# Token-major v projection with a gathered copy of n: residue copies, one warm-up matmul, one GpSimd subtraction, and a three-piece output store

## The chip, the cores and the metric

The kernel runs on one core of a Trainium2 chip. The metric is the device time of one execution in microseconds (us). Five engines work from queues of their own, each in its own order: TensorE (PE in the profile, with its weight loads as PEld), VectorE (DVE), ScalarE (ACT), GpSimd (POOL) and SyncE (SP), which only issues transfers here. SBUF is the on-chip memory of 128 partitions that all engines read; PSUM takes the results of matmuls.

## The reference

One layer of an encoder, for 512 tokens of width 1024, in float32. The part that matters here is the first norm and the combined projection, with v read out by strided subsequences for the dilated attention groups.

```python
n = rms_norm(h, norm_mix_pre[l])
proj = jnp.einsum('bsd,de->bse', n, w_in[l])
z_gmlp, q, k, v, gates = jnp.split(proj, split_points, axis=-1)
...
def strided(t):
    return t.astype(jnp.float32).reshape(B, L, dilation, H, Dh).transpose(0, 2, 1, 3, 4)
...
h = h + rms_norm(mix_out, norm_mix_post[l])
n2 = rms_norm(h, norm_mlp_pre[l])
hid = jnp.square(jax.nn.relu(jnp.einsum('bsd,df->bsf', n2, w_up[l])))
mlp_out = jnp.einsum('bsf,fd->bsd', hid, w_down[l])
h = h + rms_norm(mlp_out, norm_mlp_post[l])
```

There are three v groups of 512 columns. The first belongs to plain window attention; the second and the third are needed token by token within the residues r = 0..3 of the position modulo 4.

## The kernel before

**Arithmetic.** Every float32 product is made of three matmuls (`mm3`, lines 84 to 86): each operand is split into a high part (a rounded copy, made by ScalarE) and a low part (the difference, made by VectorE), and high x high, high x low and low x high are summed in PSUM.

**The start (lines 123 to 225).** x comes in four blocks of 128 tokens, shifted by 64 positions, in the order 1, 2, 3, 0. `square_x` takes the sum of squares of a block on ScalarE (line 169), `norm_x` scales the block on VectorE (`xn`, line 176), TensorE turns it in two groups of four transposes (`pt`, line 180), ScalarE copies the result into `nh` (line 182) and VectorE makes `nl` (line 183). So `nh` and `nl` hold n with the feature on the partition and the token along the row. Meanwhile the eight slabs of the first v group's weights are split: `w0hi` on ScalarE (line 193), `w0lo` on VectorE, for k = 3 and 7 on GpSimd (line 194). Each block then takes 24 matmuls into `pv`, 96 in all, and `pv` is split into `v0h` and `v0l`. Three unused matmuls (`idle`, line 153) and the two that spread the norm's gain (`pgn`, line 158) run before.

**The second and third v groups (`token_major`, lines 235 to 247, called at line 277).** For g = 0 and 1 and each residue r, the stationary operand is `n[:, k, ROT + r:ROT + S:4]`: 128 tokens, four apart, so that a partition reads 128 float32 numbers that stand 16 bytes apart. Each g takes 8 x 4 x 3 = 96 matmuls; the weights come as `slab` and are split into `hi` and `lo` (lines 74 and 75). Between them `four_sums` builds the sums of n that a later stage needs (`nf`, `sum`). The same `token_major` with unstrided stationary operands is used later for another column group.

**After that** come the projections of q and k for each head (`pf`), which take `nh` and `nl` as the moving operand, with the rotary part in `rope_tile`: the constants `rope`, `masks`, `perm`, `rows` and `wsp` are loaded through GpSimd's queue. Then follow the attention, the gates, the output projection and the feed-forward part.

**The end (lines 957 to 969).** For each of four blocks of tokens the last matmuls are followed by `post_norm`: squares on ScalarE (line 727), a small chain over VectorE and GpSimd for the scale, the products `y` (line 730), two sums of 128x512 into `o` (line 732), and two stores of 256 KB.

**What sets the order.** A scheduler fixes the order of each engine's instructions when the program is built; `tc.issue_after` adds constraints. At run time an engine that waits holds up everything behind it in its queue; only weight loads run ahead. Pools are stacked in SBUF: a pool that opens where another has closed waits for the last readers of the tiles it overlays.

Of the kernel before, what the change touches and what calls it, by code (L numbers as in the profile page):

```python
# [10 lines left out]
F32 = mybir.dt.float32  # L11
F32R = mybir.dt.float32r
AF = mybir.ActivationFunctionType
ALU = mybir.AluOpType
PSUM = bass.MemoryType.PSUM

P = 128
S = 512
D = 1024
KD = D // P  # L20
# [7 lines left out]
GW = 512  # L28
COL_U, COL_V = 0, GW
COL_Q, COL_K, COL_VV, COL_G = 1024, 2560, 4096, 5632  # L30
ROT = 64
# [5 lines left out]
def block_kernel(ctx: ExitStack, tc: tile.TileContext, x, norm_mix_pre, w_in, b_gate, ln_v_gain, ln_v_bias,  # L37
                 w_spatial, b_spatial, w_branch_a, w_branch_b, w_out, norm_mix_post, norm_mlp_pre, w_up,
                 w_down, norm_mlp_post, ident_c, rope_c, mask_c, perm_c, out):
    nc = tc.nc  # L40
    x, out, w_in, w_up, w_down, w_out = x[0], out[0], w_in[0], w_up[0], w_down[0], w_out[0]
    w_branch_a, w_branch_b, w_spatial = w_branch_a[0], w_branch_b[0], w_spatial[0]

    def pool(stack, name, bufs=1, space=None, side=None):
        kw = {"side": side} if side else {}
        if space is not None:
            kw["space"] = space
        return stack.enter_context(tc.tile_pool(name=name, bufs=bufs, reuse_waits="tile", **kw))
# [9 lines left out]
    onesq = consts.tile([P, P], F32, name="onesq")  # L58
# [47 lines left out]
    nh = npool.tile([P, KD, S + ROT], F32R, name="nh")  # L106
    nl = npool.tile([P, KD, S + ROT], F32R, name="nl")
# [3 lines left out]
    nat = slice(ROT, ROT + S)  # L111
# [7 lines left out]
    start = ExitStack()  # L119
# [3 lines left out]
    blocks = [1, 2, 3, 0]  # L123
# [18 lines left out]
    xts = [load_x(blocks[0])]  # L142
# [8 lines left out]
    for _ in range(3):  # L151
        idle = psA.tile([P, P], F32, name="idle", tag="acc", bufs=4)
        spun = nc.tensor.matmul(idle, onesq, onesq, start=True, stop=True)
    pgain = []
    for hf in range(2):
        pgn = psA.tile([P, 512], F32, name="pgn", tag=("y", "T")[hf])
        with tc.issue_after(spun.ins):
            spun = nc.tensor.matmul(pgn, onesq[:1], grow[:, hf * 512:(hf + 1) * 512], start=True, stop=True)
        pgain.append(pgn)

    def square_x(b, xt):
        junk = xpool.tile([P, D], F32, name="junk", bufs=1)
        ss = small.tile([P, 2], F32, name="ss")
        for hf in range(2):
            hs = slice(hf * 512, (hf + 1) * 512)
            if hf and b == blocks[0]:
                nc.vector.tensor_tensor_reduce(junk[:, hs], xt[:, hs], xt[:, hs], 1.0, 0.0, ALU.mult, ALU.add, ss[:, 1:2])
            else:
                sq = nc.scalar.activation(junk[:, hs], xt[:, hs], AF.Square, accum_out=ss[:, hf:hf + 1])
        return rstd_of(ss, 1.0 / D), sq  # L170
# [18 lines left out]
    def split_w0(k):  # L189
        raw = w0raw[k // 2][:, k % 2]  # L190
        hi = w0pool.tile([P, GW], F32R, name="w0hi")
        lo = w0pool.tile([P, GW], F32R, name="w0lo")
        ins = nc.scalar.activation(hi, raw, AF.Copy)
        (nc.gpsimd if k in (3, 7) else nc.vector).tensor_tensor(lo, raw, hi.bitcast(F32), op=ALU.subtract)
        w0.append((hi, lo))
        return ins

    rs = {0: square_x(blocks[0], xts[0])[0]}
    scaled, hi, lo = norm_x(blocks[0], xts[0], rs[0])
# [3 lines left out]
    with tc.issue_after(hi.ins):  # L203
        for k in range(2, 4):
            ins = split_w0(k)
        with tc.issue_after(ins.ins):
            rs[1], sq = square_x(blocks[1], xts[1])
        with tc.issue_after(sq.ins):
            for k in range(4, KD):
                ins = split_w0(k)  # L210
        with tc.issue_after(ins.ins):
            rs[2], sq = square_x(blocks[2], xts[2])
    for i in range(4):
        if i + 1 < 4:
            _, hi, lo = norm_x(blocks[i + 1], xts[i + 1], rs[i + 1])
        if i == 0:
            with tc.issue_after(hi.ins):
                rs[3], _ = square_x(blocks[3], xts[3])
        b = blocks[i]
        pv = psA.tile([P, GW], F32, name="pv", tag="acc", bufs=4)  # L220
        for k in range(KD):
            sl = slice(b * P, (b + 1) * P)
            mm3(pv, (nh[:, k, sl], nl[:, k, sl]), w0[k], k == 0, k == KD - 1)
        split_into(v0h[:, b], v0l[:, b], pv)
# [10 lines left out]
    def token_major(c0, stationary, evac, half_way=None):  # L235
        accs = [psA.tile([P, 512], F32, name="pv", tag="acc", bufs=4) for _ in range(4)]
        for k0, raw in slabs(w_in, c0, KD, 512, 4):
            if k0 and half_way:
                half_way()
            for j in range(0, 4, 2):  # L240
                wh, wl = wsplit(raw[:, j:j + 2])
                for jj in range(2):
                    k = k0 + j + jj
                    for r in range(4):
                        mm3(accs[r], (stationary(nh, k, r), stationary(nl, k, r)), (wh[:, jj], wl[:, jj]), k == 0, k == KD - 1)
        for r in range(4):
            evac(r, accs[r])
# [6 lines left out]
    def four_sums():  # L254
        with ExitStack() as st:
            spool = pool(st, "spool")
            f = spool.tile([P, KD, S], F32, name="nf")
            for k in range(0, KD, 2):
                nc.vector.tensor_tensor(f[:, k:k + 2], nhn[:, k:k + 2].bitcast(F32), nln[:, k:k + 2].bitcast(F32), op=ALU.add)
            fe, fo = f[:, 0:KD:2], f[:, 1:KD:2]  # L260
            nc.vector.tensor_tensor(fe[:, :, A], fe[:, :, A], fe[:, :, B], op=ALU.subtract)
            nc.vector.tensor_tensor(fe[:, :, B], fo[:, :, B], fe[:, :, B], op=ALU.subtract)
            nc.vector.scalar_tensor_tensor(fo[:, :, B], fe[:, :, A], -1.0, fo[:, :, B], op0=ALU.mult, op1=ALU.subtract)
            nc.vector.scalar_tensor_tensor(fo[:, :, A], fo[:, :, B], -1.0, fo[:, :, A], op0=ALU.mult, op1=ALU.subtract)
            for n, part in ((6, fo[:, :, B]), (5, fe[:, :, A]), (7, fe[:, :, B]), (4, fo[:, :, A])):
                hl = spool.tile([P, 2, KH, 256], F32R, name="sum", bufs=4)
                split_into(hl[:, 0], hl[:, 1], part)
                nc.gpsimd.dma_start(sums[n], hl)

    for g in range(2):  # L270
        def ev(r, ps, g=g):
            if r % 2:
                nc.vector.tensor_copy(v12[:, g, r], ps)
            else:
                nc.scalar.activation(v12[:, g, r], ps, AF.Copy)
        with tc.issue_after(hi.ins), tc.issue_after(lo.ins):
            token_major(COL_VV + (g + 1) * GW, lambda n, k, r: n[:, k, ROT + r:ROT + S:4], ev)
        if g == 0:
            four_sums()

    def feature_tile(wh, wl, nk, mh, ml, tag="acc"):
        ps = psA.tile([P, S], F32, name="pf", tag=tag, bufs={"acc": 4, "S": 2, "T": 1, "y": 1}[tag])
# [19 lines left out]
    for i, (vec, n) in enumerate(((b_gate, 16), (ln_v_gain, 4), (ln_v_bias, 4), (norm_mlp_pre, 8))):  # L302
        o = (0, 16, 20, 24)[i]
# [284 lines left out]
    for g2 in range(2):  # L588
        raw = wload([KD, 2 * P], lambda r: [(r, fcols(w_in, COL_U + g2 * 2 * P, KD, 2 * P))], "uw")
        for j in range(2):  # L590
            g = 2 * g2 + j
            wh, wl = wsplit(raw[:, :, j * P:(j + 1) * P], sub=nc.gpsimd)
            ps = psA.tile([P, S], F32, name="pf", tag="acc" if g else "T", bufs=4 if g else 1)
            for k in range(KD):
                ins = mm3(ps, (wh[:, k], wl[:, k]), (nhn[:, k], nln[:, k]), k == 0, k == KD - 1)
# [12 lines left out]
            t = gpool.tile([P, 4, P], F32, name="sv", bufs=2)  # L608
# [72 lines left out]
    for d in range(GSTD):  # L681
        g2 = gate_rows(d - GSTD)
        raw = gate_raw(d)
# [23 lines left out]
    gain = hpool.tile([P, D], F32, name="gain", bufs=1)  # L707
    nc.gpsimd.dma_start(gain, norm_mix_post.to_broadcast([P, D]))
    h2d = tc.dram_tile([S, D], F32, name="h2d")
    halves = [slice(0, 512), slice(512, 1024)]  # L710
# [10 lines left out]
    def all_banks():  # L721
        return [[psB.tile([P, 512], F32, name="pd", tag=tg, bufs=4) for _ in range(2)] for tg in ("tp", "tp", "acc", "acc")]

    def post_norm(pss, gain, ys, dst, res, junk):
        ss = small.tile([P, 2], F32, name="ss2")
        for hf, hs in enumerate(halves):
            nc.scalar.activation(junk[hf], pss[hf].rearrange("p (k c) -> p k c", c=P), AF.Square, accum_out=ss[:, hf:hf + 1])
            if hf:
                r = rstd_of(ss, 1.0 / D)
            nc.vector.tensor_tensor(ys[hf], pss[hf], gain[:, hs], op=ALU.mult)  # L730
        for hf, hs in enumerate(halves):
            nc.vector.scalar_tensor_tensor(dst[:, hs], ys[hf], r, res[:, hs], op0=ALU.mult, op1=ALU.add)

    wo = ExitStack()
    wopool = pool(wo, "wopool", bufs=5)
# [35 lines left out]
    for t in range(4):  # L771
        ts_ = slice(t * P, (t + 1) * P)
# [58 lines left out]
    for i in range(1, NSTD):  # L831
        raw = raw_up(i)
# [126 lines left out]
    for t in range(4):  # L959
        ts_ = slice(t * P, (t + 1) * P)  # L960
        h2 = n2pool.tile([P, D], F32, name="h2", tag="n2")
        nc.gpsimd.dma_start(h2, h2d[ts_])
        for hf in range(2):
            for f, hh, hl, wh, wl in last:
                down(t, f, hf, hh, hl, wh, wl)
        o = lpool.tile([P, D], F32, name="o", bufs=2)
        post_norm(accs[t], gain, [lpool.tile([P, 512], F32, name="y", bufs=2) for _ in range(2)], o, h2, [o[:, hs].rearrange("p (k c) -> p k c", c=P) for hs in halves])
        for hs in halves:
            nc.sync.dma_start(out[t * P:(t + 1) * P, hs], o[:, hs])
    dn.close()  # L970
    back.close()

# [38 lines left out]
```

## Time and profile before

| | us |
|---|---|
| median of 3 runs | 814.18 |
| lowest and highest | 813.3 and 814.45 |
| the profiled execution's own time | 814.04 |
| its span, first to last instruction | 812.3 |
| PE busy in the span | 801.9 |
| ACT busy in the span | 371.6 |

The profiled execution took 1.74 us more than its span shows, for what lies around it. The mean granted clock of TensorE was 0.999. A timeline row gives the start, the duration, the engine, the line, the operation with the tiles it writes and reads, the count, and in brackets how long the engine had been idle before and what released it. A row of the groups gives the count, then the total busy time in us and the mean of one in ns, then the idle time before.

### The profile page before, as it was taken

The page shows a single profiled execution, that of the slowest core. Times are in us where ns is not written, and L with a number is a line of the kernel's source. Part 1 is how long each engine was busy: PE and PEld are TensorE (multiplying, and loading weights), DVE is VectorE, ACT ScalarE, POOL GpSimd, SP SyncE. Part 2 cuts the span into 40 slices and gives each one's busy share as a digit, 9 for nine tenths or more (in the row PEclk, how much of TensorE's full clock was granted, in tenths as well). Part 3 has the DMA queues.
Part 4 walks back from the last instruction along what each step waited for, and adds up shares of the span by engine and source line. Part 5 has one row for each costly group of instructions (what it writes and reads, how often), then busy time and mean ns, then how long its engine had stood idle before and what let it go on. Part 6 is the DMA issues. An engine that isn't in the chain of part 4 may idle for free.

```text
span 812.3 us, 11650 instructions
## 1 busy us (share of the span) xinstructions
PE 801.9 (99%) x4629; PEld 711.8 (88%) x4629; DVE 546.8 (67%) x916; ACT 371.6 (46%) x609; POOL 85.4 (11%) x92
## 2 busy tenths in 40 slices
PE   8999999999999999999999999999999999999996
PEld 5899888888888889999988899999999888888885
DVE  6772788978783978788656579988887533333324
ACT  6342334434344545454535447666676522332212
POOL 2012113232222400000000200000000000000000
PEclk9999999999999999999999999999999999999999
DMA  9367333232131283244446223333334632332202
GB/s 294 123 228 187 98 104 104 53 90 67 52 104 53 65 284 105 79 112 122 130 137 227 103 79 94 114 105 104 106 108 144 235 109 103 104 104 77 79 1 104
DMA packets 83960, 95.34 MB, mean 117 GB/s; under 512 B 2417, under 2 KB 70033, under 8 KB 82882
## 3 DMA queue, kind: packets, MB, share of 16 engines
q1 hardware_dynamic: 80208, 77.60, 31.5%
q0 software_dynamic: 3696, 17.00, 6.0%
q8 instruction: 36, 0.59, 0.3%
q14 instruction: 18, 0.15, 0.1%
q10 hardware_dynamic: 2, 0.00, 0.0%
HBM read 86.20 MB, written 8.39 MB: 116 GB/s over the span
## 4 chain that ended last, share of the span: by engine, by line
PE 94%; DMA 2%; DVE 2%; ACT 1%; SPq 0%; issue 0%; DVEq 0%; POOLq 0%; ACTq 0%
PE pacc L880 12%; PE pd L85 9%; PE pd L84 9%; PE pd L86 9%; PE pf L86 9%; PE pf L85 9%; PE pf L84 9%; PE pgacc L555 6%; PE ptp L880 4%; PE pv L84 4%; PE pv L85 3%; PE pv L86 3%; PE pgS L555 2%; DMA xt<-in_x_dram 1%; PE psb L373 1%; PE py L485 1%
## 5 line engine op out<-in xcount | busy, mean ns | idle before, releaser
L84 PE MATMUL pf<-nh,hi 128*128 128x512 f32 x240 | 94.6, 394 | 0.0
L85 PE MATMUL pf<-nl,hi 128*128 128x512 f32 x240 | 94.5, 394 | 0.0
L86 PE MATMUL pf<-nh,lo 128*128 128x512 f32 x240 | 94.2, 392 | 0.0
L85 PE MATMUL pd<-hl,hh 128*128 128x512 f32 x224 | 87.2, 389 | 0.0
L84 PE MATMUL pd<-hl,hh 128*128 128x512 f32 x224 | 86.2, 389 | 0.0
L86 PE MATMUL pd<-hl 128*128 128x512 f32 x224 | 86.0, 389 | 0.0
L80 DVE TENSOR_TENSOR hl<-hid,hh 128x512 fp32r<-128x512 f32 x28 | 19.2, 693 | 75.6 <-ACT hh L79 75.6
L880 PE MATMUL pacc<-nt,hl 128*128 128x256 f32 x504 | 67.7, 280 | 0.1
L880 PEld LDWEIGHTS pacc<-nt,hl 128*128 128x128 f32 x504 | 62.7, 188 | 0.4 <-ACT hl L79 0.3
L79 ACT ACTIVATE hh<-hid 128x512 fp32r<-128x512 f32 x28 | 17.4, 630 | 89.0 <-PE pd L85 89.0
L314 POOL TENSOR_TENSOR sw<-sw,rope 32x512 f32<-32x512 f32 x24 | 41.9, 1745 | 131.7 <-DVE sw L312 114.6
L86 PEld LDWEIGHTS pf<-nh,lo 128*128 128x128 f32 x240 | 45.1, 188 | 8.9
L84 PEld LDWEIGHTS pf<-nh,hi 128*128 128x128 f32 x240 | 45.1, 188 | 8.7
L85 PEld LDWEIGHTS pf<-nl,hi 128*128 128x128 f32 x240 | 45.1, 188 | 8.6
L86 PEld LDWEIGHTS pd<-hl 128*128 128x128 f32 x224 | 42.0, 188 | 8.8
L84 PEld LDWEIGHTS pd<-hl,hh 128*128 128x128 f32 x224 | 42.0, 188 | 8.7
L85 PEld LDWEIGHTS pd<-hl,hh 128*128 128x128 f32 x224 | 42.0, 188 | 8.5
L80 DVE TENSOR_TENSOR hl<-dnw,hl 128x1024 fp32r<-128x1024 f32 x32 | 39.1, 1225 | 13.9 <-ACT hl L79 13.9
L74 ACT ACTIVATE hi<-qkw 128x1024 fp32r<-128x1024 f32 x24 | 25.4, 1058 | 49.3 <-PE pf L85 25.5
L880 PE MATMUL pacc<-n,hl 128*128 128x256 f32 x336 | 45.2, 280 | 0.4 <-ACT z L905 0.4
L75 DVE TENSOR_TENSOR lo<-qkw,hi 128x1024 fp32r<-128x1024 f32 x24 | 36.9, 1538 | 12.1 <-ACT hi L74 11.5
L79 ACT ACTIVATE hl<-s 128x1024 fp32r<-128x1024 f32 x28 | 29.6, 1058 | 29.1 <-DVE s L864 10.8
(317 smaller groups left out, 1992.3 us busy)
## 6 DMA issues: line engine op xcount, KB each, us to landing
upw<-in_w_up_dram SPq DMA_DIRECT2D x16, 1024.0 KB, 5.5
dnw<-in_w_down_dram SPq DMA_DIRECT2D x16, 1024.0 KB, 4.9
qkw<-in_w_in_dram SPq DMA_DIRECT2D x24, 512.0 KB, 5.3
gw<-in_w_in_dram SPq DMA_DIRECT2D x16, 512.0 KB, 5.4
slab<-in_w_in_dram SPq DMA_DIRECT2D x6, 1024.0 KB, 9.8
sum<-sum POOLq DMA_DIRECT2D x4, 1024.0 KB, 7.8
nt<-sum POOLq DMA_DIRECT2D x4, 1024.0 KB, 8.0
wow<-in_w_out_dram SPq DMA_DIRECT2D x4, 1024.0 KB, 4.8
```

What stands on the lines that cost most here:

```text
L74: nc.scalar.activation(hi, raw, AF.Copy)
L75: (sub or nc.vector).tensor_tensor(lo, raw, hi.bitcast(F32), op=ALU.subtract)
L79: nc.scalar.activation(hi, src, AF.Copy)
L80: return nc.vector.tensor_tensor(lo, src, hi.bitcast(F32), op=ALU.subtract)
L84: nc.tensor.matmul(ps, ah, bh, start=start, stop=False)
L85: nc.tensor.matmul(ps, ah, bl, start=False, stop=False)
L86: return nc.tensor.matmul(ps, al, bh, start=False, stop=stop)
L314: nc.gpsimd.tensor_tensor(sw, sw, rope[:, 1], op=ALU.mult)
L373: nc.tensor.matmul(ps[:, rr, g - 1], got["q", g][:, r], got["k", g][:, r], start=True, stop=True)
L485: nc.tensor.matmul(o, v12[:, g, r, hs], ptb[r // 2][:, r % 2, g], start=False, stop=(r == 3 and g == 1), skip_group_check=True)
L555: nc.tensor.matmul(ps, a[:, j], b[:, j], start=first and not (j or i), stop=(j == KH - 1 and i == 2), skip_group_check=True)
L880: nc.tensor.matmul(ps, a[:, j], b[:, j], start=first and not (j or m), stop=(j == KH - 1 and m == 2), skip_group_check=True)
```

## The change

Five edits:

- One more unused matmul of 128x128 is issued after the two `pgn` matmuls.
- The low part of w0 for k = 5 is made by GpSimd instead of VectorE, as those for k = 3 and 7 already were.
- The squares of the third block are no longer issued ahead of the second block's `nh` copies; they follow them, with the fourth block's.
- A pool `rpool` opens after the start's pools have closed and holds `nr`, 128 x 2 x 8 x 4 x 128 float32 (32 KB a partition): `nh` and `nl` with the tokens sorted by residue. Eight copies of 128x1024 on ScalarE, each over two k, read `n` with a step of four numbers and write `nr` unbroken. `token_major` of the second and third v groups takes its stationary operands from `nr`. The pool closes after them, so the tiles placed there later (`rope` and the other constants among them) wait for the last of these matmuls.
- In the last stage the second half of the output block is summed in two pieces of 128x256 and each of the three pieces is stored as soon as it is there.

```diff
     for hf in range(2):
         ...
         pgain.append(pgn)
+    with tc.issue_after(spun.ins):
+        spun = nc.tensor.matmul(idle, onesq, onesq, start=True, stop=True)
...
-        (nc.gpsimd if k in (3, 7) else nc.vector).tensor_tensor(lo, raw, hi.bitcast(F32), op=ALU.subtract)
+        (nc.gpsimd if k in (3, 5, 7) else nc.vector).tensor_tensor(lo, raw, hi.bitcast(F32), op=ALU.subtract)
...
-        with tc.issue_after(ins.ins):
-            rs[2], sq = square_x(blocks[2], xts[2])
     for i in range(4):
         if i + 1 < 4:
             _, hi, lo = norm_x(blocks[i + 1], xts[i + 1], rs[i + 1])
         if i == 0:
             with tc.issue_after(hi.ins):
-                rs[3], _ = square_x(blocks[3], xts[3])
+                for j in (2, 3):
+                    rs[j], _ = square_x(blocks[j], xts[j])
...
+    res = ExitStack()
+    nr = pool(res, "rpool").tile([P, 2, KD, 4, P], F32R, name="nr")
+    for k in range(0, KD, 2):
+        for z, n in enumerate((nh, nl)):
+            nc.scalar.activation(nr[:, z, k:k + 2], n[:, k:k + 2, nat].bitcast(F32).rearrange("p k (l r) -> p k r l", r=4), AF.Copy)
...
-            token_major(COL_VV + (g + 1) * GW, lambda n, k, r: n[:, k, ROT + r:ROT + S:4], ev)
+            token_major(COL_VV + (g + 1) * GW, lambda n, k, r: nr[:, 0 if n is nh else 1, k, r], ev)
         if g == 0:
             four_sums()
+    res.close()
...
-        for hf, hs in enumerate(halves):
-            nc.vector.scalar_tensor_tensor(dst[:, hs], ys[hf], r, res[:, hs], op0=ALU.mult, op1=ALU.add)
+        parts = [slice(0, 512), slice(512, 1024)] if out is None else [slice(0, 512), slice(512, 768), slice(768, 1024)]
+        for hs in parts:
+            hf = hs.start // 512
+            nc.vector.scalar_tensor_tensor(dst[:, hs], ys[hf][:, hs.start - 512 * hf:hs.stop - 512 * hf], r, res[:, hs], op0=ALU.mult, op1=ALU.add)
+            if out is not None:
+                nc.sync.dma_start(out[:, hs], dst[:, hs])
```

ScalarE's queue at the passage from the start to the second v group (the lines with a plus are those of the changed kernel, in which every line number is a little higher; `hi<-slab` are the high parts of that group's weights, `v0h` the first group's results, `sum` those of `four_sums`):

```order
 L74 ACTIVATE hi<-slab 128x1024 [waits DMAHW3_49]
-L185 ACTIVATE nh<-nh 128x8x64 [waits Activation_49]
-L79 ACTIVATE v0h<-pv 128x512 [waits PE_49] x2
+L187 ACTIVATE nh<-nh 128x8x64 [waits Activation_49]
+L275 ACTIVATE nr<-nl 128x1024 [waits DVE_49,Pool_49]
+L275 ACTIVATE nr<-nl 128x1024 x3
+L79 ACTIVATE v0h<-pv 128x512 [waits PE_49]
+L275 ACTIVATE nr<-nh 128x1024 [waits Activation_49]
+L275 ACTIVATE nr<-nh 128x1024 x3
+L79 ACTIVATE v0h<-pv 128x512 [waits PE_49]
 L79 ACTIVATE sum<-nf 128x1024 [waits DVE_49]
```

The eight copies stand behind the three slab splits, all four of `nl` first, then one `v0h`, then the four of `nh`. On TensorE the first matmul of the second v group, `pv<-hi,nr`, stands as before straight behind the last one of the first group, and now waits for the first copy of `nh`.

TensorE's queue in the start, where the second block is turned (`pt`) while the first block's matmuls (`pv`) run:

```order
 L84 MATMUL pv<-w0hi,nh 128x512
-L180 MATMUL pt<-ident,xn 128x128 x8
+L182 MATMUL pt<-ident,xn 128x128 x4
+L85 MATMUL pv<-w0lo,nh 128x512
+L86 MATMUL pv<-w0hi,nl 128x512
+L84 MATMUL pv<-w0hi,nh 128x512
+L182 MATMUL pt<-ident,xn 128x128 x4
 L85 MATMUL pv<-w0lo,nh 128x512
```

The second group of four transposes has moved behind three matmuls, the first of which needs the low part that GpSimd now makes.

ScalarE's queue a little later in the start, before the change (`junk` is a square, here of the third block; `nh` the copies of the second):

```order
L193 ACTIVATE w0hi<-w0raw 128x512 [waits DMAHW6_49]
L193 ACTIVATE w0hi<-w0raw 128x512
L169 ACTIVATE junk,ss<-xt 128x512 [waits DMAHW7_49,Activation_49]
L169 ACTIVATE junk,ss<-xt 128x512
L182 ACTIVATE nh<-pt 128x4x128 [waits PE_49] x2
```

and with the change:

```order
L195 ACTIVATE w0hi<-w0raw 128x512 [waits DMAHW6_49]
L195 ACTIVATE w0hi<-w0raw 128x512
L184 ACTIVATE nh<-pt 128x4x128 [waits PE_49] x2
L171 ACTIVATE junk,ss<-xt 128x512 [waits DMAHW7_49,Activation_49]
L171 ACTIVATE junk,ss<-xt 128x512
```

The copies of the second block now stand ahead of the squares, which wait for a transfer.

More of the change, by code (lines that the diff above doesn't have):

```diff
@@ L722, in all_banks, with post_norm @@
         return [[psB.tile([P, 512], F32, name="pd", tag=tg, bufs=4) for _ in range(2)] for tg in ("tp", "tp", "acc", "acc")]
-    def post_norm(pss, gain, ys, dst, res, junk):
+    def post_norm(pss, gain, ys, dst, res, junk, out=None):
         ss = small.tile([P, 2], F32, name="ss2")
@@ L966, in block_kernel @@
         o = lpool.tile([P, D], F32, name="o", bufs=2)
-        post_norm(accs[t], gain, [lpool.tile([P, 512], F32, name="y", bufs=2) for _ in range(2)], o, h2, [o[:, hs].rearrange("p (k c) -> p k c", c=P) for hs in halves])
-        for hs in halves:
-            nc.sync.dma_start(out[t * P:(t + 1) * P, hs], o[:, hs])
+        post_norm(accs[t], gain, [lpool.tile([P, 512], F32, name="y", bufs=2) for _ in range(2)], o, h2, [o[:, hs].rearrange("p (k c) -> p k c", c=P) for hs in halves], out[ts_])
     dn.close()
```

## The prediction

> **What bounds the kernel now.** The page comes first.
>
> ```profile
> PE 801.9 (99%) x4629; PEld 711.8 (88%) x4629; DVE 546.8 (67%) x916; ACT 371.6 (46%) x609; POOL 85.4 (11%) x92
> PE 94%; DMA 2%; DVE 2%; ACT 1%; SPq 0%; issue 0%; DVEq 0%; POOLq 0%; ACTq 0%
> ```
>
> TensorE is busy for 99% of the span and makes 94% of the chain that ended last. So an edit gains only if it removes matmul time or one of the few waits of TensorE, and it loses whatever it lets TensorE wait. The windows by stage show where waits are.
>
> ```profile
> 9.00:20.00 11.00, 9.81 (x39) 7.41 (x39) 8.87 (x17) 9.19 (x22) 3.73 (x4) 1.00 1.05 319
> 37.40:60.00 22.60, 22.60 (x98) 22.60 (x98) 17.02 (x16) 8.80 (x10) 2.21 (x4) 1.00 0.59 208
> ```
>
> Columns after the window are its length and the busy time of PE, PEld, DVE, ACT and POOL. From 9 to 20 us TensorE idles for 1.2 us and ScalarE works 9.2 of 11 us. From 37.4 to 60 us, the strided v group, TensorE never idles, and the weight loads never do either: 22.60 of 22.60.
>
> **The strided loads: what the copy can bring.** Groups by form, and the first and last timeline rows of two runs of matmuls:
>
> ```profile
> L84 PEld LDWEIGHTS pv<-hi,nh 128*128 128x128 f32 x64 | 19.4, 310 | 0.0
> L84 PEld LDWEIGHTS pf<-nh,hi 128*128 128x128 f32 x66 | 12.4, 188 | 2.5
> 37.43 0.40 PE L84 MATMUL pv<-hi,nh 128*128 128x512 f32 x1
> 82.55 0.40 PE L84 MATMUL pf<-nh,hi 128*128 128x512 f32 x1
> ...
> 91.86 0.39 PE L86 MATMUL pf<-nh,lo 128*128 128x512 f32 x1
> ```
>
> A strided load takes 310 ns, an unbroken one 188. The 192 strided matmuls start from 37.43 to 82.55: 45.12 / 192 = 235.0 ns each. The next 41, with unbroken loads, take 9.31 / 41 = 227.1 ns. Reading `nr` makes the loads unbroken: 192 x 7.9 ns = **1.5 us gained**. If the pitch had another cause, nothing.
>
> **The copies: what they cost.** They stand on ScalarE between the slab splits and the first strided matmul:
>
> ```profile
> 29.87 0.60 ACT L182 ACTIVATE nh<-pt 128x512 fp32r<-128x512 f32 x1 [2.59 <-PE pt L180]
> 30.36 2.95 ACT L74 ACTIVATE hi<-slab 128x1024 fp32r<-128x1024 f32 x3
> 33.21 0.62 ACT L185 ACTIVATE nh<-nh 128x512 fp32r<-128x512 f32 x1
> 33.73 0.59 ACT L79 ACTIVATE v0h<-pv 128x512 fp32r<-128x512 f32 x1
> 37.63 0.60 ACT L79 ACTIVATE v0h<-pv 128x512 fp32r<-128x512 f32 x1 [3.32 <-PE pv L86]
> 44.48 3.90 ACT L79 ACTIVATE sum<-nf 128x1024 fp32r<-128x1024 f32 x4 [6.24 <-DVE nf L263]
> ```
>
> By totals there is room: 3.32 + 6.24 us idle for eight copies of about 1 us. The order decides otherwise. The queue runs four copies of `nl`, one `v0h`, and only then the copy of `nh` that the matmul at 37.43 waits for. Three splits in 2.95 us, the last of 1.06, give a start every 0.945 us. With copies as fast as these splits, the first starts at 33.73, `v0h` at 33.73 + 4 x 0.945 = 37.51, the copy of `nh` 0.49 later (33.21 to 33.73 is such a step), and it ends at 38.00 + 1.06 = 39.06. TensorE goes on at 39.1: it loses **1.7 us, the lower end**.
>
> But these copies read SBUF with a step of 16 bytes. No row shows ScalarE doing that. The nearest:
>
> ```profile
> L316 DVE TENSOR_TENSOR q<-q,sw 32x512 f32<-32x512 f32 x8 | 8.6, 1071 | 1.2 <-POOL sw L314 0.9
> L316 DVE TENSOR_TENSOR qk0t<-qk0t,sw 32x512 f32<-32x512 f32 x8 | 5.4, 677 | 0.4
> L313 ACT ACTIVATE q<-pf 128x512 f32<-128x512 f32 x8 | 4.8, 596 | 0.2
> L313 ACT ACTIVATE qk0t<-pf 128x512 f32<-128x512 f32 x8 | 4.7, 585 | 2.7 <-DVE sw L312 2.7
> ```
>
> Line 316 reads `sw` from SBUF, for `q` with the same step: 1071 against 677 ns, 0.77 ns more per number. The strided weight load reads the very numbers of this change: (310 - 188) / 128 = 0.95 ns more. Line 313 is ScalarE with that step, but out of PSUM: 596 against 585, nothing. I take the SBUF rows, since two engines agree there and the operand is the same: 1024 numbers cost 0.79 to 0.98 us more per copy. Five copies lie ahead of the matmul, so its wait is 1.7 + 5 x 0.79 = 5.6 to 1.7 + 5 x 0.98 = 6.6; **6.1 us lost**. [...]
>
> Behind the first copy nothing else is late. The next matmuls that wait need a copy each, every 12 matmuls (12 x 0.227 = 2.7 us), and a copy takes under 2 us. The matmuls that need `hi<-slab` of k = 6 come 72 later, 16.3 us, with four copies, `v0h` and the four `sum` splits ahead of it: at 1.9 us a copy VectorE would finish that slab's low part about 1 us ahead of TensorE.
>
> **TensorE after the wait.** It has begun slowly once:
>
> ```profile
> 7.13 1.97 PE L180 MATMUL pt<-ident,xn 128*128 128x128 f32 x8 [0.53 <-DVE xn L176]
> ...
> 10.38 0.63 PE L84 MATMUL pv<-w0hi,nh 128*128 128x512 f32 x1
> 10.80 0.63 PE L85 MATMUL pv<-w0lo,nh 128*128 128x512 f32 x1
> ...
> 13.02 0.40 PE L86 MATMUL pv<-w0hi,nl 128*128 128x512 f32 x1
> 13.25 0.39 PE L84 MATMUL pv<-w0hi,nh 128*128 128x512 f32 x1
> 14.18 1.15 PE L180 MATMUL pt<-ident,xn 128*128 128x128 f32 x8
> ```
>
> At 10.4 us matmuls start 0.42 apart, at 13 us 0.23; eight transposes take 1.97 and later 1.15, though the windows give a granted clock of 1.00 throughout. Seven matmuls at 0.2 more are 1.4 us, with the transposes' 0.8 it is 2.2. No wait in this trace is long enough to show whether 6 us bring this back: nothing, or 1.4 to 2.2; I take **1.8 us lost**. [...]
>
> **The start.** Three edits act on one piece:
>
> ```profile
> 12.29 0.56 POOL L96 TENSOR_TENSOR rs_out<-rs_in,neghalf 128x1 f32<-128x1 f32 x1
> 14.16 1.27 POOL L194 TENSOR_TENSOR w0lo<-w0raw,w0hi 128x512 fp32r<-128x512 f32 x1 [1.31 <-ACT w0hi L193]
> 14.47 2.10 DVE L194 TENSOR_TENSOR w0lo<-w0raw,w0hi 128x512 fp32r<-128x512 f32 x2
> 15.61 0.63 ACT L169 ACTIVATE junk<-xt 128x512 f32<-128x512 f32 x1 [1.53 <-DMA xt<-in_x_dram]
> 16.03 0.50 PE L85 MATMUL pv<-w0lo,nh 128*128 128x512 f32 x1 [0.70 <-DVE w0lo L194]
> 16.85 1.06 ACT L182 ACTIVATE nh<-pt 128x512 fp32r<-128x512 f32 x2
> 17.48 0.50 PE L84 MATMUL pv<-w0hi,nh 128*128 128x512 f32 x1 [0.49 <-ACT nh L182]
> 18.29 0.39 PE L86 MATMUL pv<-w0hi,nl 128*128 128x512 f32 x1
> ```
>
> TensorE waits 0.70 for the low part of k = 5 and 0.49 for the second block's `nh`, which stands behind squares that wait for a transfer. With the change GpSimd makes k = 5 from about 13.1 to 14.4 and k = 7 to 15.7. TensorE does four transposes at 14.18 (half of 1.15), three matmuls to 15.4, four transposes to 16.0. VectorE's low part for k = 6 meets GpSimd's as today (two took 2.10 instead of 1.4 beside GpSimd's, and ended 0.45 behind it): about 16.2. Three matmuls later, at 16.9, TensorE stands where it stood at 18.29, 22 `pv` matmuls done: 1.4 gained. `nh` is ready by 15.6. At the third block a matmul that covered the copy behind the transposes now stands ahead of them: 0.2 back. **1.2 us gained**; 0.5 if GpSimd and VectorE hold each other up more, 1.8 if the extra matmul, which lies in the 0.53 us of idle time before 7.13, also ends the slow start sooner. ScalarE's chain behind the last transposes shifts by the same amount, so the wait above stays as it is.
>
> **The constants.** `rope` now waits for the last strided matmul.
>
> ```profile
> 62.16 0.59 POOL L298 DMA_DIRECT2D rope<-in_rope_c_dram  x1 [11.08 <-DMA sum<-sum]
> 89.03 1.27 POOL L314 TENSOR_TENSOR sw<-sw,rope 32x512 f32<-32x512 f32 x1 [21.98 <-DVE sw L312]
> 104.33 0.61 PE L373 MATMUL psb<-k,q 128*128 128x128 f32 x4
> ```
>
> Queued behind it on GpSimd are seven more transfer issues; they lasted from 62.16 to 67.05, 4.9 us. From 82.7 that is 87.6, 1.4 before `sw` is wanted, and what `sw` feeds is first read at 104.33. Cost nothing; a delay has 15 us of cover.
>
> **The end.**
>
> ```profile
> 807.23 1.41 DVE L732 SCALAR_TENSOR_TENSOR o<-y,rs_out,h 128x512 f32<-128x512 f32 x2
> out_dram<-o SPq DMA_DIRECT2D x6, 256.0 KB, 2.0
> ```
>
> The last sum ends about 0.1 later as two pieces, and the last store is half as long. **0.1 us gained**, between 0.2 lost and 0.4 gained.
>
> **The sum**, from the profiled execution's own 814.04: - 1.5 - 1.2 + 6.1 + 1.8 - 0.1 = **819.1 us**. That execution lies 0.14 below the median of the runs shown, which is within what this sum can tell.
>
> **The rivals.**
>
> 1. *Not slower: ScalarE reads the strided rows at its usual rate.* Then the wait is 1.7, too short for a slow phase (waits of 0.7 left none): 814.04 - 1.5 - 1.2 + 1.7 - 0.1 = **812.9**. For it: line 313, and ScalarE may have a better path than VectorE. Against: both SBUF rows. It decides by the copy's length: the gains sum to 2.8, so the wait may be 2.8, a copy of 1.06 + (2.8 - 1.7) / 5 = 1.3 us; below that the change gains.
> 2. *The wait, but no slow phase*: 819.1 - 1.8 = **817.3**. For it: the clock column reads 1.00 even in the slow start, so what ended that start is not seen.
> 3. *The strided load does not set the pitch*, so the copy brings nothing: 819.1 + 1.5 = **820.6**. Against it: PEld is full in the strided window only.
>
> **How the numbers follow.** Forecast 0.60, rival 1 0.14, rival 2 0.18, rival 3 0.04, something between rivals 1 and 2 (copies slowed by less than half) 0.04. The forecast's own range is 817.5 to 820.8, from the bounds of the wait (5.6 to 6.6), the slow phase (1.4 to 2.2) and the start (0.5 to 1.8). The forecast and rival 2 alone hold 0.78, and the lower bound of the copy's cost belongs in the range, so it runs from 812.5 to 821.0. A measurement of this kernel tells about 0.2%, 1.6 us, from no change. Rival 1 lies 0.14% below before, so mostly within that: faster 0.05, the same 0.14, slower 0.81.
>
> **What would show it.** In the changed trace: ScalarE's copies `nr<-nl` at 1.8 to 2.0 us each (rival 1: 1.06); TensorE idle 5.6 to 6.6 us before the first `pv<-hi,nr`, released by ScalarE; the matmuls behind it 0.42 apart for some 3 to 4 us (rival 2: 0.23); later `pv<-hi,nr` 0.227 apart with loads of 188 ns; the first v group's last matmul about 1.2 us earlier than now. The forecast is wrong if the copies are quick, or if the start gains or loses several us.

## The result and the profile after

| | before | after |
|---|---|---|
| median, us | 813.74 (4 runs) | 821.32 (4 runs) |
| lowest and highest | 813.26 and 814.45 | 820.36 and 822.54 |
| the profiled execution's own time | 814.04 | 821.76 |
| its span | 812.3 | 820.0 |
| mean granted clock | 0.999 | 0.993 |

The changed kernel is slower: 1.0093 of the time, 95% interval 1.0076 to 1.0111. The forecast was 819.1 with a range up to 821.0, so the direction was right and the time lies 0.3 above the range.

ScalarE's queue after the change, in the timeline (start, duration, engine, line, operation, count):

```profile
32.81 7.90 ACT L275 ACTIVATE nr<-nl 128x1024 fp32r<-128x1024 f32 x4
40.59 0.60 ACT L79 ACTIVATE v0h<-pv 128x512 fp32r<-128x512 f32 x1
41.06 7.89 ACT L275 ACTIVATE nr<-nh 128x1024 fp32r<-128x1024 f32 x4
48.80 0.64 ACT L79 ACTIVATE v0h<-pv 128x512 fp32r<-128x512 f32 x1
```

Four copies of `nl`, one split, then `nh`: the order of the prediction, at 7.90 / 4 = 1.98 us a copy. TensorE at the same place:

```profile
36.28 0.39 PE L86 MATMUL pv<-w0hi,nl 128*128 128x512 f32 x1
43.19 0.80 PE L84 MATMUL pv<-hi,nr 128*128 128x512 f32 x1 [6.52 <-ACT nr L275]
43.78 0.63 PE L85 MATMUL pv<-lo,nr 128*128 128x512 f32 x1
44.21 0.63 PE L86 MATMUL pv<-hi,nr 128*128 128x512 f32 x1
...
47.62 0.51 PE L85 MATMUL pv<-lo,nr 128*128 128x512 f32 x1
47.97 0.40 PE L86 MATMUL pv<-hi,nr 128*128 128x512 f32 x1
48.21 0.39 PE L84 MATMUL pv<-hi,nr 128*128 128x512 f32 x1
...
89.01 0.39 PE L84 MATMUL pf<-nh,hi 128*128 128x512 f32 x1
```

The wait is 6.52 us, and the matmuls behind it stand 0.43 apart until 47.97. The windows of 1 us show why (length, busy time and count of PE, PEld, DVE, ACT and POOL, then the granted clock, DMA share and GB/s):

```profile
40.00:41.00 1.00, 0.00 (x0) 0.00 (x0) 0.00 (x0) 1.00 (x2) 0.00 (x0) 1.00 0.00 0
41.00:42.00 1.00, 0.00 (x0) 0.00 (x0) 0.77 (x2) 1.00 (x2) 0.00 (x0) 0.52 0.00 0
...
47.00:48.00 1.00, 1.00 (x4) 0.77 (x4) 0.00 (x0) 1.00 (x2) 0.00 (x0) 0.56 0.00 0
48.00:49.00 1.00, 1.00 (x6) 0.83 (x5) 0.00 (x0) 1.00 (x2) 0.00 (x0) 1.00 0.00 0
```

TensorE was granted half its clock from shortly after 41 to shortly before 48: 0.96 + 5 + 0.88 = 6.8 us, by 0.52 and 0.56 at the edges and 0.50 in each window between.

The stretch from the first group's last matmul to the first `pf` matmul, 193 matmuls, takes 89.01 - 36.28 = 52.73 us. Before it took 82.55 - 37.20 = 45.35. It is 7.4 longer: 6.5 of wait, less 192 x (235.0 - 226.7) ns = 1.6 for the unbroken loads (the 181 matmuls from 47.97 take 41.04 us, 226.7 ns each), and the remaining 2.5 for the half clock and the restart.

The rest of the 7.7 us by which the spans differ lies at three places: 0.9 gained before 36.28, 0.9 lost in the up-projection (the offset is 6.5 us when its first matmul starts and 7.4 when the down-projection's does), 0.3 lost at the end.

### The profile page after: what moved, and what is told of

The parts are those of the page before. It is cut to its first block, busy times and chain, and to the rows that moved or that the text cites. A ratio compares the mean times of both kernels' runs of the same rounds, so it can differ in the third digit from the quotient of the medians.

```text
span 820.0 us, 11674 instructions
## 1 busy us (share of the span) xinstructions
PE 803.4 (98%) x4631; PEld 704.9 (86%) x4631; DVE 547.2 (67%) x919; ACT 386.9 (47%) x617; POOL 86.9 (11%) x93
## 4 chain that ended last, share of the span: by engine, by line
PE 92%; DVE 3%; ACT 3%; DMA 1%; issue 0%; POOLq 0%; POOL 0%; DVEq 0%; ACTq 0%
PE pacc L892 11%; PE pd L85 9%; PE pd L86 9%; PE pd L84 9%; PE pf L86 9%; PE pf L85 8%; PE pf L84 8%; PE pgacc L563 6%; PE ptp L892 4%; PE pv L85 3%; PE pv L84 3%; PE pv L86 3%; PE pgS L563 2%; ACT nr L275 1%; PE psb L381 1%; PE py L493 1%
```

## The experiments

Each ratio is against the kernel before, run on the same chip in the same job.

**e1: everything but the sorted copy.** The eight copies and their pool are left out, and the stationary operands come from `n` again:

```diff
-            token_major(COL_VV + (g + 1) * GW, lambda n, k, r: nr[:, 0 if n is nh else 1, k, r], ev)
+            token_major(COL_VV + (g + 1) * GW, lambda n, k, r: n[:, k, ROT + r:ROT + S:4], ev)
```

> The kernel after without the sorted copy: the second and third v groups load their strided slices of nh and nl again; the other four edits stay. Theory (the copies cost 6.5 of wait and 2.1 of slow phase and bring 1.5; the start brings 0.9, the end loses 0.2): no wait on nr, v-group matmuls 0.235 apart again, first pf matmul at 81.7, 813.7 - 0.9 + 0.2 = 813.0, or 813.9 if the up-projection's period (10.05 before, 10.12 after) stays long. Rival (the loss is not from the copies but from the other edits): 819 or more.

Measured: 814.43 us (813.33 to 814.69, 11 runs), ratio 0.9997 (0.9988 to 1.0006). No wait on ScalarE's copies, first `pf` matmul at 81.82. The whole loss of the change comes and goes with the copy; the other four edits together make no difference that these runs resolve.

**e2: the sorted copy alone**, put into the kernel before.

> The kernel before with the sorted copy alone. Theory: a wait of about 6.5 on ScalarE's copy, a phase at half clock of about 2.1, v-group matmuls 0.227 apart behind it: 813.7 + 6.5 + 2.1 - 1.5 = 820.8, and up to 0.9 more if the up-projection's matmuls run at their longer spacing. Rival (the other edits carry most of the loss): under 817.

Measured: 820.61 us (819.24 to 823.15, 6 runs), ratio 1.0080 (1.0067 to 1.0093). Its list of waits (total, times, longest, in us):

```profile
PE pv L84 <- ACT nr L274: 6.5, 1, 6.5
```

As expected, in its size too.

**e3: the copies by pairs of k.** `prev` is the last instruction of the queue ahead.

```diff
+    prev = hi
     for k in range(0, KD, 2):
         for z, n in enumerate((nh, nl)):
-            nc.scalar.activation(nr[:, z, k:k + 2], ...)
+            with tc.issue_after(prev.ins):
+                prev = nc.scalar.activation(nr[:, z, k:k + 2], ...)
```

> The kernel after with its eight copies held in the order in which the code names them, nh and nl by turns from the first pair of k, where the kernel after has all four of nl first. Theory (what costs is that five copies stand ahead of the first matmul, not the copies' 15.8 us on ScalarE): the first pv matmul on nr waits under 0.7, no stretch at half clock, first pf matmul at 80.4 to 81.0, 821.3 - 6.5 - 2.1 + (0 to 0.7) = 812.7 to 813.4. Rival (ScalarE's 15.8 us are the price in any order, since later matmuls, the weights' high parts and the sums queue behind them): the waits come back further on, 816 or more.

Measured: 818.45 us (817.45 to 819.4, 5 runs), ratio 1.0051 (1.0039 to 1.0063): 2.9 less than the kernel after, not 8, and in the rival's range. Waits, the windows of 1 us and ScalarE's timeline:

```profile
PE pv L84 <- DVE v0l L80: 2.0, 1, 2.0
PE pv L85 <- DVE lo L75: 0.9, 1, 0.9
```

```profile
50.00:51.00 1.00, 0.89 (x3) 0.71 (x4) 1.00 (x2) 0.00 (x0) 0.00 (x0) 0.90 0.00 0
51.00:52.00 1.00, 1.00 (x4) 0.78 (x3) 0.97 (x2) 0.00 (x0) 0.00 (x0) 0.50 0.00 0
...
54.00:55.00 1.00, 1.00 (x5) 0.85 (x4) 1.00 (x2) 1.00 (x2) 0.00 (x0) 0.90 0.00 0
```

```profile
46.86 2.00 ACT L277 ACTIVATE nr<-nl 128x1024 fp32r<-128x1024 f32 x1
48.77 0.57 ACT L79 ACTIVATE v0h<-pv 128x512 fp32r<-128x512 f32 x1
```

The wait on the copies is gone and another stands in its place. The first v group's last result sits in the bank of PSUM (one of the four buffers that hold a result of 128x512) that the second group's fourth tile needs. Its split `v0h`, whose matmuls were done at about 37, now stands behind all eight copies. TensorE waits 2.0 us, until 50.1, for the low part of that split. From 50.8 on it is granted half clock, for 0.2 + 3 + 0.2 = 3.4 us (0.50 in each window from 51 to 54). So the order of `nl` and `nh` was only a part of it. Whether ScalarE has room at all for the copies, which the rival denied, e13 below answers: with the same eight copies nothing of this is left. In the kernel after, the same split was just as late (48.80), and the slow phase hid it.

**e4: the wait kept, TensorE kept busy in it.**

```diff
...
+    idle2 = psA.tile([P, 512], F32, name="idle2", tag="y")
+    for _ in range(28):
+        with tc.issue_after(last_pv.ins):
+            last_pv = nc.tensor.matmul(idle2, nh[:, 0, :P], nh[:, 0, :S], start=True, stop=True)
...
```

> The kernel after with 28 unused 128x512 matmuls put into TensorE's wait for the copy (28 x 0.227 = 6.4 us). Theory (the slow phase comes from TensorE's idle time, as the granted clock of 0.50 from 41 to 48 us says): the copies end when they did, matmuls behind them 0.227 apart from the first, no granted clock under 1.00, 821.3 - 2.1 = 819.2. Rival (the matmuls are slow because the strided copies still running on ScalarE take their turn at the memory): still 0.42 apart to about 47.6, 821.3.

Measured: 820.29 us (820.16 to 821.09, 5 runs), ratio 1.0074 (1.0061 to 1.0087). The timeline of TensorE:

```profile
43.19 0.50 PE L84 MATMUL pv<-hi,nr 128*128 128x512 f32 x1 [0.22 <-ACT nr L275]
43.53 0.40 PE L85 MATMUL pv<-lo,nr 128*128 128x512 f32 x1
43.76 0.39 PE L86 MATMUL pv<-hi,nr 128*128 128x512 f32 x1
...
50.13 0.50 PE L84 MATMUL pv<-hi,nr 128*128 128x512 f32 x1 [1.21 <-DVE v0l L80]
```

The copy ends when it did, but the matmuls behind it run 0.23 apart from the second on, beside the same copies on ScalarE, and the granted clock from 36 to 50 us is 1.00, where the kernel after has 0.76. So the slow phase comes from TensorE's idle time, not from the copies' accesses. It saves only 89.01 - 88.34 = 0.7 at the first `pf` matmul, since the faster matmuls reach the late split: 1.2 us of wait that the slow phase had covered. (From here on this is called the bank's wait.)

**e7 and e8: what makes a copy slow.** In e7 the copies read in a row and write in a row, so they sort nothing. In e8 they read in a row and sort in what they write, with a step of 512 bytes.

```diff
-nc.scalar.activation(nr[:, z, k:k + 2], n[:, k:k + 2, nat].bitcast(F32).rearrange("p k (l r) -> p k r l", r=4), AF.Copy)
+nc.scalar.activation(nr[:, z, k:k + 2], n[:, k:k + 2, nat].bitcast(F32).rearrange("p k (r l) -> p k r l", r=4), AF.Copy)
...
+nc.scalar.activation(nr[:, z, k:k + 2].rearrange("p k r l -> p k l r"), n[:, k:k + 2, nat].bitcast(F32).rearrange("p k (l r) -> p k l r", r=4), AF.Copy)
```

> The kernel after with the eight copies reading rows of 512 in a row instead of every fourth element; same count, size and order. This leaves the sorting by residue out: the second and third v groups are those of other tokens. Theory (the step of 16 bytes between read elements is the price): copies 0.95 to 1.06 us apart, first pv matmul on nr after a wait of 6.5 - 5 x 0.98 = 1.6, no half clock there, 821.3 - 4.9 - 2.1 = 814.3. Rival (the copy is slow for its size, its write or its place beside VectorE's work): copies still 1.95 apart, 821.3.

> The kernel after with the eight copies walking both tiles in the order of nh's and nl's columns: still every element of a row in turn, so reads are 4 bytes apart and writes 512 bytes apart. Theory that only a step in the reads costs: 0.95 to 1.06 us a copy, wait 1.6, 814.3. Theory that a step on either side costs: 1.95 us a copy or more, wait 6.5 or more, 821.3 or more.

Measured, one run each: 813.53 and 821.73 us. ScalarE's timeline in e7, and then in e8:

```profile
32.75 3.89 ACT L275 ACTIVATE nr<-nl 128x1024 fp32r<-128x1024 f32 x4
```

```profile
32.82 7.57 ACT L275 ACTIVATE nr<-nl 128x1024 fp32r<-128x1024 f32 x4
```

A copy takes 3.89 / 4 = 0.97 us without a step, 1.98 with a step of 16 bytes on the read side, 1.89 with a step of 512 bytes on the write side. The step is the price in these two runs, on either side: 1.0 and 0.9 us more for 1024 numbers. Why a step costs this, and what one of another size would cost, no run shows. e7's wait was 1.5 us, at a mean granted clock of 0.997 over the execution, as in e4; e8's was 6.1 us, at 0.994, as in e2 and e11.

**e5 and e6: all orders set.** The copies by pairs; the last first-group split ahead of the second pair's copies; the fourth high part of the weights ahead of the sums; on TensorE each pair's first tile behind the pair ahead. e6 also has the old end in two pieces.

```diff
-        split_into(v0h[:, b], v0l[:, b], pv)
+        split_0 = nc.scalar.activation(v0h[:, b], pv, AF.Copy)
+        nc.vector.tensor_tensor(v0l[:, b], pv, v0h[:, b].bitcast(F32), op=ALU.subtract)
...
+            with tc.issue_after(prev.ins), tc.issue_after((split_0 if k else prev).ins):
+                prev = nc.scalar.activation(nr[:, z, k:k + 2], ...)
...
+                with tc.issue_after(split_w[-1].ins):
                     split_into(hl[:, 0], hl[:, 1], part)
...
+                            if r == 0 and k % 2 == 0 and k:
+                                behind.enter_context(tc.issue_after(ins.ins))
                             mm3(accs[r], ...)
```

> The kernel after with four orders set: the copies by pairs of k, nh and nl by turns; the last first-group block's split ahead of the copies of the second pair; on TensorE each pair's matmuls for all four tiles ahead of the next pair's; on ScalarE the last high part of the weights ahead of the four sums. Theory (each wait seen so far is an order on ScalarE: five copies ahead of the first matmul in the kernel after, the split behind all eight copies in the run with the copies by pairs): no wait over 0.5 on TensorE between 36 and 80 us, granted clock 1.00 there, first pf matmul at 80.0 to 80.8, time 813.9 - 0.9 - 1.5 + (0 to 0.7) + 0.3 = 811.8 to 812.5. Rival (ScalarE has no room for 15.8 us of copies in 44 us of v groups, so some other work of it comes late): a wait of 2 us or more and with it half clock, 815 or more.

> As the run with the four orders set, and the last sum and store in two pieces as in the kernel before. Theory (from the last matmul's start to the end of the span it was 7.36 us in the kernel after, 7.08 before): 0.3 less than that run, 7.1 from the last matmul to the end, 811.5 to 812.2. Rival (three pieces bring the 0.1 of the prediction, and the 0.28 is the spread of single runs): 7.4 or more, and 0.1 slower.

Both came out slower than expected. Measured: e5 813.59 us (813.3 to 814.66, 11 runs), ratio 0.9999 (0.9990 to 1.0008); e6 812.84 us (812.69 to 813.82, 11 runs), ratio 0.9991 (0.9982 to 1.0000). What TensorE still waits for in e5:

```profile
PE pv L88 <- ACT nr L284: 0.9, 2, 0.7
```

These two waits are 0.9 of the 1.6 us of the unbroken loads, and the rest of the gain is gone too, at a place that these rows do not show: from the first group's last matmul to the first `pf` matmul e5 takes 45.38 us, the kernel before 45.35. Matmuls of a later pair ran ahead of the fourth tile's and came to the copies too early; with whole pairs in order (e9, below) no wait on `nr` is left. The end: from the start of the last matmul to the end of the span it is 6.65 us in e6 and 7.35 in e5, so the third piece costs 0.7 here, where 0.3 was expected.

**e9 and e13: whole pairs in order on TensorE**, in e9 wherever the helper is used, in e13 in the second and third v groups alone. The lines are those of e13 against e6; e9 does not have `and whole`.

```diff
-                            if r == 0 and k % 2 == 0 and k:
-                                behind.enter_context(tc.issue_after(ins.ins))
+                            if done and whole:
+                                behind.enter_context(tc.issue_after(done.ins))
```

> As the run with the four orders and the end in two pieces, but on TensorE all matmuls of a pair of k, not only those of the first tile, stand behind the pair ahead of it. Theory (the two waits left there, 0.3 and 0.9 us by the spacing of the matmuls, are matmuls of the second and third pair that run ahead of the fourth tile's and so reach the copies too early; a pair is 24 x 0.227 = 5.4 us of TensorE against 3.95 of copies): no wait on nr over 0.2, first pf matmul at 80.1 to 80.6 instead of 81.7, 1.1 to 1.6 less than that run's 812.8 (its lower group of times): 811.2 to 811.7, or 1.0 more in the upper group. Rival (another thing comes late, the fourth high part of the weights or the fourth tile's bank): a wait of 0.5 or more, 812.5 or more.

> As the run with whole pairs in order on TensorE, but that order set in the second and third v groups alone, not in the later product of the same helper, between 237 and 264 us. Theory (the sorted copy is worth its 1.6 us where nothing waits for it; what that run lost, 2.35 us between the first pf matmul and 309 us, came from the later product's order, which moved the matmuls of attention): first pf matmul at 80.5 to 80.9, offset of the same size (1.0 to 1.1 earlier than in the run with the end in two pieces) kept to the end, 811.5 to 811.9 in the lower group of times, median 811.5 to 812.9, ratio about 0.998. Rival (attention loses it whenever the v groups end 1 us earlier): the wait of 1.7 on ptal comes again, 814.

Measured: e9 814.52 us (814.14 to 816.63, 11 runs), ratio 1.0013 (1.0003 to 1.0023). That is slower than e6, where a gain was expected. No wait on `nr` is left and the first `pf` matmul comes at 80.65, but this wait in attention is new:

```profile
PE pt L479 <- DVE ptal L82: 1.7, 1, 1.7
```

e13: 811.94 us (811.6 to 812.88, 11 runs), ratio **0.9982 (0.9973 to 0.9991)**. The wait on `ptal` is gone, so e9's loss came from the order set in the later product. The first `pf` matmul of e13, its last matmul, and the waits on the v groups' matmuls:

```profile
80.89 0.39 PE L86 MATMUL pf<-nh,hi 128*128 128x512 f32 x1
...
803.53 0.39 PE L88 MATMUL pd<-hl,hhl 128*128 128x512 f32 x1
```

```profile
PE pv L86 <- DVE v L290: 0.3, 1, 0.3
PE pv L86 <- ACT nh L186: 0.3, 1, 0.3
```

Against e6 the first `pf` matmul is 0.8 earlier, and so is the start of the last matmul (803.53 against 804.35): a gain of the v groups reaches the end. From the first group's last matmul to the first `pf` matmul e13 takes 44.50 us, against 45.35 in all four profiles with strided loads (before, e1, e10, e12). So the sorted copy gains 0.85 there, of the 1.6 of the loads. That is not all of what e13 gains against the kernel before: the edits of the start are in it too, and its end is 0.4 shorter (6.64 against 7.08), for which no cause is shown. e13 is faster than both kernels.

**e10: the three edits of the start alone**, in the kernel before. The diff is that of the change.

> The kernel before with the three edits of the start alone: the extra unused matmul, the sixth low part on GpSimd, the squares of the third block behind the second block's copy. Theory (the start brings 0.7 to 0.9, as the first pf matmul of the run without the sorted copy said, 81.82 against 82.55): first pf matmul at 81.6 to 81.9, 6.65 from the last matmul to the end, 0.7 to 0.9 less than the kernel before. Rival (the gain was a chance of one execution): no difference, 82.5.

Measured: 813.24 us (812.99 to 814.43, 11 runs) against 813.45, ratio 0.9996 (0.9987 to 1.0005). The first `pf` matmul comes at 81.56, as expected, but from the last matmul to the end it is 7.07 us and not 6.65. A gain of 0.7 to 0.9 in the time is neither shown nor excluded.

**e11 and e12: the kernels after and before once more.**

> The kernel after once more. Theory (the up-projection's matmuls take one of two spacings in each execution, whatever the kernel): either 117.8 ns as before in this kernel, or 116.7, and then the offset against the kernel before stays at 6.5 us behind the up-projection and the time is 1.0 less, 820.7; the times fall in two groups about 1 us apart. Rival (the change makes the spacing longer): 117.8 again and no time under 821.

> The kernel before once more, for the same question. Theory: 116.7 or 117.8 ns in the up-projection, with 813.2 or 814.1 to 814.4. Rival: 116.7 in every execution of this kernel, and the two groups of its times (813.2 and 814.2) come from elsewhere.

Measured: e11 821.17 us (820.69 to 821.25, 4 runs), e12 one run, 814.3. The up-projection in equal windows of 80 us, first of the kernel after (first profile, then e11), then of the kernel before (first profile, then e12):

```profile
542.50:622.50 80.00, 80.00 (x682) 80.00 (x681) 66.71 (x95) 52.19 (x73) 0.00 (x0) 1.00 0.35 106
```

```profile
542.50:622.50 80.00, 80.00 (x688) 80.00 (x687) 67.41 (x97) 52.58 (x73) 0.00 (x0) 1.00 0.35 106
```

```profile
536.00:616.00 80.00, 80.00 (x688) 80.00 (x688) 67.42 (x97) 52.98 (x74) 0.00 (x0) 1.00 0.34 106
```

```profile
536.00:616.00 80.00, 80.00 (x681) 80.00 (x680) 67.29 (x97) 52.86 (x74) 0.00 (x0) 1.00 0.34 106
```

688 matmuls or 681 to 682 in the same time, never idle: 116.3 or some 117.4 ns each by these counts, in either kernel. The rest of the profiles bear this out without a count. From the first `pf` matmul to the program's last matmul it is 722.6 to 722.7 us in ten profiles (before, e11, e1, e2, e3, e5, e6, e7, e10, e13) and 723.6 to 723.7 in four (after, e12, e4, e8); e9, with its wait in attention, stands apart. So the 0.9 us that the first pair of profiles shows here is not the change's; the rival is out. The rest of the expectation did not hold: e11's times form no two groups, and its profiled execution has the short spacing and yet takes 821.25. There the half clock came 0.9 later (the window from 41 to 42 has 0.97, that of the first profile 0.52) and so covered more of the matmuls, until 48.8, as this window says:

```profile
48.00:49.00 1.00, 1.00 (x4) 0.77 (x4) 0.00 (x0) 1.00 (x2) 0.00 (x0) 0.62 0.00 0
```

Its first `pf` matmul comes at 89.45 instead of 89.01, after the same wait of 6.51. The start differs between executions too. In e12, the kernel before, the first group's last matmul starts 0.8 earlier than in that kernel's first profile (37.20):

```profile
36.42 0.40 PE L86 MATMUL pv<-w0hi,nl 128*128 128x512 f32 x1
```

With the old start it stands at 37.20, 36.42 and 37.22 (e2), with the new one between 36.15 and 36.47 in all twelve profiles. ScalarE's rows in e12 say why:

```profile
13.95 0.62 ACT L169 ACTIVATE junk<-xt 128x512 f32<-128x512 f32 x1
...
15.18 1.06 ACT L182 ACTIVATE nh<-pt 128x512 fp32r<-128x512 f32 x2
```

In the first profile the squares began at 15.61 and the `nh` copies behind them at 16.85, after a wait of 1.53 us for the transfer of the third block of x; e2 has a wait of 1.33 there. In e12 they begin at 13.95 and 15.18, with no such wait. So what the moved squares are worth hangs on when that transfer lands.

## Why the prediction was right in direction and 2 us short

The path was as predicted: the copies on ScalarE hold TensorE up, and it goes on slowly behind them. What failed are sizes. The slow phase was put at 1.8 us and cost 2.5 to 2.9, since the half clock lasted 6.8 us. The start was put at 1.2 gained and brought 0.9 in one pair of profiles and 0.1 in the other. The wait was 0.4 longer than predicted, the end lost 0.3 where 0.1 was to be gained, and the spread of the up-projection was no term of the sum.

The first pair is before and after, the second e12 and e11; all in us.

| step | predicted | in the profiles |
|---|---|---|
| unbroken loads | -1.5 | -1.6 |
| wait for the copy | +6.1 | +6.5 |
| slow phase | +1.8 | +2.5 with the restart, +2.9 in the second pair |
| start | -1.2 | -0.9 in the first pair, -0.1 in the second |
| end | -0.1 | +0.3 |
| up-projection | none | +0.9 in the first pair, -1.0 in the second |
| sum, and the difference of the spans | +5.1 | +7.7 and +6.9 |

- **The strided loads set the spacing**: right. Rival 3 is out: 226.7 ns against 235.0. What was put against it, that PEld is full in the strided window only, does not hold: in the up-projection of the kernel before it is busy for 80.00 of 80.00 us.
- **The copies are slow on ScalarE**: right, and e7 shows that the step is the cause. Rival 1 (copies at the usual rate) gave 812.9; with copies in a row it was 813.5. It took its wait of 1.7 as too short for a slow phase, from waits of 0.7; half clock came in a wait of 2.0 (e3) and not in one of 1.2 (e4), and none of 1.7 was run. The size was a little low: a step costs 1.0 us a copy, above the two rows of SBUF (0.79 and 0.98), of which the middle was taken. Five times 1.0 on e7's wait of 1.5 is the 6.5 measured.
- **Slow matmuls behind the wait**: right; rival 2 is out. The slow starts of the prediction were the wrong scale (1.4 to 2.2). The granted clock, which read 1.00 there, shows the phase here plainly: from 43.2 to 47.9, 4.7 us of matmuls at half clock lose half of that, 2.35. The half clock lasted 6.8 us, of which 2.2 fell into the wait itself. It did not come at one distance from the last matmul ahead of the wait: 4.4 us after that one's end in the kernel after, 5.2 in e11, after the same wait, and 2.7 in e3.
- **Nothing else is late**: right for the kernel after only by luck: the slow phase covered the bank's wait. The prediction followed what a matmul needs of the copies and the weights, and not the bank that a split must free on the same engine. e3 and e4 met it at once.
- **The start, 1.2 gained**: this step failed. Its waits (0.53, 0.49, 0.70) were read from one execution, and the 0.49 hung on a transfer that came 1.53 us late for ScalarE there. e12 shows the unchanged kernel without that wait and its first group done 0.8 earlier. So the edits gain 0.9 against the one execution and 0.1 against the other. They keep `nh` from waiting for the transfer, which fits the narrow 36.15 to 36.47 of the new start. In the times the gain is not resolved: e10's interval reaches from 1.1 us faster to 0.4 slower.
- **The end, 0.1 gained**: failed, with the sign. From the start of the last matmul to the end of the span it is 7.34 to 7.38 us in the profiles with three pieces, 7.07 to 7.08 with two where n is not sorted, 6.64 to 6.66 where it is; why sorting shortens it is not shown. The last sums take 1.54 instead of 1.41 and a third issue stands behind them:

```profile
812.60 0.39 PE L86 MATMUL pd<-hl,hhl 128*128 128x512 f32 x1
814.63 1.54 DVE L742 SCALAR_TENSOR_TENSOR o<-y,rs_out,h 128x512 f32<-128x512 f32 x3
```

- **The range**: its upper end added the bounds of wait, slow phase and start, but took the profiled execution's other stages as fixed. Two of them, the start and the up-projection, vary by 0.8 and 1.0 us between executions of one kernel. e1's, e5's and e6's times fall in two groups about 1 us apart. With the new start the first group's end varies by only 0.3, so the up-projection is the likelier cause; but the profiled executions of all three are of the lower group and have the short spacing, so this is not shown.

## What to carry to other kernels

The copy that sorts an operand moved the price of the step here from the engine that reads it often (235.0 to 226.7 ns a matmul) to the one that copies it once (1.98 us a copy instead of 0.97); it paid only where the copies reached the reader in the order in which it reads, and the orders made most of the difference between 0.9% lost and 0.2% gained (8.6 of the 9.4 us from the kernel after to e13; the end in two pieces made the rest). Follow a busy engine's queue not only for what the waiting engine reads but for the splits that free its banks (2.0 us of wait in e3). Before a term is read from a wait of half a microsecond, look at a second execution of the same kernel, and at what the wait hangs on.

## What the runs showed of the hardware

- Half clock, 0.50 in the windows, was granted for 6.8 us in the kernel after (wait of 6.52 us), until 48.8 in e11 (6.51) and for 3.4 us in e3 (2.02); in e4, with a wait of 1.21, the windows have 1.00. The mean over the execution is 0.994 in e2 and e8, with waits of 6.5 and 6.1, as in e11, and 0.997 in e7, with 1.5, as in e4. So a wait of 2.0 us was enough in e3; what sets when the half clock begins and how long it lasts, no run shows.
- ScalarE kept to its queue's order: in the profile of before the `nh` copies, whose transposes were done at 15.33 us, began at 16.85, behind squares that had waited 1.53 us for a transfer. Of TensorE's instructions a weight load ran ahead of its matmul: that of the matmul at 37.43 us began at 37.21.
- ScalarE pays for a step out of SBUF what it did not pay out of PSUM in the profile of before: 1.98 against 0.97 us for 128x1024 with a step of 16 bytes (596 against 585 ns for 128x512 out of PSUM), and nearly as much, 1.89, for a step of 512 bytes in what it writes.
- The up-projection's matmuls, with TensorE and its loads busy all the time, run at one of two spacings 1% apart in executions of the same kernel (116.3 and some 117.4 ns); what picks the spacing stays open.
